# Six small constant tiles allocated ahead of the two token operands, which moves the operands by 224 bytes in every partition

## The chip, the cores and the metric

The kernel runs on one core of one Trainium2 chip. The metric is the device time in microseconds (us) of one execution; the time before is 2092.78 us, the median of three runs from 2089.54 to 2096.44 us.

## What is computed

One transformer block on 256 tokens of width 2048, all in float32: a modulation vector from a conditioning row (`mod = silu(c) @ ada_w + ada_b`, six pieces), a normed and modulated mixer, and a normed and modulated expert layer.

```
h = rms_norm(x, norm_mix_g) * (1 + sc1) + sh1
x = x + gt1 * hybrid_mixer(h, ...)      # attention (3 branches) + gated linear recurrence
h = rms_norm(x, norm_ffn_g) * (1 + sc2) + sh2
x = x + gt2 * peer_ffn(h, ...)          # 16384 experts: gelu(h @ down.T) * gate, then @ up
```

The expert layer of the kernel is dense: it multiplies all tokens with all 16384 rows of `down` and `up` and sets the gates of experts that were not picked to zero.

## The kernel before

**Operands in halves.** A float32 matrix product is made of three float32r products (`mm3`, L345 to L348): both operands are split into a high and a low half (`split`, L196 to L198: ScalarE makes the high half, VectorE the low one), and high times high, high times low and low times high are added up in PSUM. In `T.matmul(o, ah, bh)` the second argument is the stationary operand, which TensorE loads into the array ahead of the product (LDWEIGHTS in the profile), and the third is the moving one, which streams through it. The stationary operand is always a block of 128 tokens: 128 columns of 4 bytes, 512 contiguous bytes in each partition. The moving one is 512 columns of split weights (`wh`, `wl`).

**Two families of stationary tiles.** `xH` and `xL` (L116, L117) hold the halves of what the next product needs of all tokens, 16 chunks of 256 tokens, and are refilled three times: with the first norm's result, the mixer's output and the second norm's result. They are the stationary operands of the first projections (PSUM tiles `f`, `a`, `r`, `xg`), of the mixer's output projection (`y`), of the experts' queries (`wq`) and of the experts' down products (`d`, 32 blocks). The up products (`u`) read other stationary tiles, `ah` and `al` (L1228, L1229), which hold the gated activations of one block of 512 experts; there are four buffers of each.

**The stream.** Weights arrive in the order of one list, a megabyte at a time (`raw`, on SP's queue), are split into `wh` and `wl` and go to TensorE in that order; beside the stream run small jobs, one step per part. A down block is 96 matmuls, an up block 48. The first 14 down blocks run with the search for the picked experts and with the building of their gates (`w`, L1184, eight small matmuls at a time) between their parts; the other 18 down blocks take turns with up blocks and have nothing between.

**Places in SBUF.** The pool `cp` has one buffer per tile, and its tiles lie one behind the other in the order in which they are allocated, each rounded up to 32 bytes per partition. `con`, `sm`, `row`, `cb`, `mod` and `cs` come first, then `xH` and `xL` (16384 bytes per partition each), then `spl`, `nsp` and `hb` (L392 to L394), and the three tiles that `softplus` makes, `e8`, `s8` and `q8` (L397 to L399). In the built program `xH` begins at byte 32576 of each partition and `xL` at 48960; both are 320 modulo 512. Each block of 128 tokens is 512 bytes, so every stationary block of `xH` and `xL` begins at 320 modulo 512. The buffers of `ah` lie from byte 170016 and those of `al` from byte 186400, in steps of 4096: 32 modulo 512, all of them. The buffers of `wh` and `wl` begin at 32 modulo 512 too, but for two of each that serve in the first projections alone and begin at 96.

Of the kernel before, what the change touches and what calls it, by code (L numbers as in the profile page):

```python
# [7 lines left out]
F32 = mybir.dt.float32  # L8
# [7 lines left out]
P = 128  # L16
# [8 lines left out]
RB = 8  # L25
# [40 lines left out]
def kernel(  # L66
# [24 lines left out]
    V, A, T, G = nc.vector, nc.scalar, nc.tensor, nc.gpsimd  # L91
# [22 lines left out]
    mod = cp.tile([P, 6, NDC], F32, name="mod")  # L114
    cs = cp.tile([P, NDC], F32, name="cs")
    xH = cp.tile([P, NDC, S], F32R, name="xH")  # L116
    xL = cp.tile([P, NDC, S], F32R, name="xL")  # L117
# [9 lines left out]

# [1 line left out]
    items = []  # L129
# [11 lines left out]
    for ch in STREAM.replace(" ", ""):  # L141
# [6 lines left out]
        else:  # L148
            src, o = wid[ch].pop(0)
# [27 lines left out]
    def load(most=RAWB):  # L177
        """Loads the stream ahead, as far as the rings allow."""
        while pos["load"] < len(items):
            it = items[pos["load"]]  # L180
            if len(raws) >= most:
                return
            t = wp.tile([P, D], F32, tag="raw", bufs=RAWB, name="raw")
            if it[0] == "ada":
                nc.sync.dma_start(t, ada_w[ada_w.shape[0] - NDC + it[1]])
            elif it[0] == "adp":
                nc.sync.dma_start(t, ada_p[it[1]])
            elif it[0] == "cmp":
                nc.sync.dma_start(t, cmp_w[it[1]][:, it[2] * D:(it[2] + 1) * D])
            else:  # L190
                n = it[2] * it[3]
                nc.sync.dma_start(t[:, 0:n], it[1])
            raws.append(t)
            pos["load"] += 1
# [5 lines left out]
    def ada_load():  # L200
        """Loads ahead, as far as the rings allow."""
        n = pos["adl"]
        if n < ada_w.shape[0] - NDC:
            own = n >= 2 * NDC or n < ADO and n % (ADAB + ADA1) < ADAB
            if sum(o == own for o, _ in avs) < (ADAB if own else ADA1):
                if own:
                    t = vp.tile([P, D], F32, tag="av", bufs=ADAB, name="av")
                else:
                    t = xp.tile([P, D], F32, tag="av1", bufs=ADA1, name="av1")
                nc.sync.dma_start(t, ada_w[n])  # L210
                avs.append((own, t))
                pos["adl"] += 1
                return True
        return False

    def ada(m):
        """One chunk of a modulation vector: rows of the turned weights times the conditioning."""
        t = avs.pop(0)[1]
        V.scalar_tensor_tensor(out=t, in0=t, scalar=1.0, in1=cb, op0=OP.mult, op1=OP.mult, accum_out=m)  # L219
        n = pos["adl"]  # L220
        while (pos["adl"] < 2 * NDC or n - len(avs) > 2 * NDC) and ada_load():
            pass

    def ada_close(seg, k, n):
        """The biases; where it scales, one plus it, times the norm's gain."""
        m = mod[:, seg, k:k + n]
# [7 lines left out]
    def bg(r):  # L234
        """A share r of a chunk of the modulation vectors that VectorE makes beside the rest."""
        bgn[1] += r
# [13 lines left out]
    def adp_item():  # L250
        """A chunk of the rows of one modulation vector, in four column groups of the array."""
        i = items[pos["take"]][1]
# [20 lines left out]
    def next_part():  # L273
        """Emits the next part of the stream; False at its end."""
        if pos["take"] >= (pos["end"] or len(items)):
# [38 lines left out]

# [1 line left out]
    jobs = []  # L316
# [13 lines left out]

    # steps per part of the stream, by the kind of work; the gate build's first steps go as fast as they may
    tk, wn = [0.0], [0]
# [7 lines left out]
    def finish(prio):  # L340
        """Runs the jobs up to that priority to their end."""
        while jobs and jobs[0][0] <= prio:
            step()
# [25 lines left out]
    def rsqrt(pool, ss, n, w, name, parts=P, bufs=2):  # L369
        """1/sqrt(ss/n + eps) of a few columns, by Newton's method from an integer first guess."""  # L370
        v = pool.tile([parts, w], F32, tag="rsv", bufs=bufs, name=f"rsv_{name}")
# [19 lines left out]

    spl = cp.tile([P, RB], F32, name="spl")  # L392
    nsp = cp.tile([P, RB], F32, name="nsp")
    hb = cp.tile([P, 2, RB], F32, name="hb")  # L394

    def softplus():
        e8 = cp.tile([P, RB], F32, name="e8")  # L397
        s8 = cp.tile([P, RB], F32, name="s8")
        q8 = cp.tile([P, RB], F32, name="q8")  # L399
        lam = sm[:, S_LAM:S_LAM + 8]  # L400
# [16 lines left out]

# [1 line left out]
    ea, e0, eq = ExitStack(), ExitStack(), ExitStack()  # L419
# [40 lines left out]
    def ada_first(n):  # L460
        """Chunks of the first two modulation vectors; the tokens' next two chunks when they are complete."""
        for _ in range(n):
# [10 lines left out]

    # two sets of four blocks, in turn over pieces of the width; the sums of the set that rests wait in SBUF
    sums = {"f": [], "a": []}
# [36 lines left out]
    def rest(b, name):  # L512
        """The rest of one of the first four blocks, added up in SBUF."""
        pst = [ps_x(f"{name}_{tb}") for tb in range(NT)]
# [17 lines left out]
    def mix(*gens, rate=0.0):  # L532
        """Steps of several pieces of work in turn."""
        gens = list(gens)
# [7 lines left out]

# [1 line left out]
    ap = ea.enter_context(tc.tile_pool(name="ap", bufs=1))  # L544
# [18 lines left out]
    vc = zp.tile([16, NG, HD], F32, name="vc")  # L563
    # the compressed branch borrows what the later branches fill
    win = oT.rearrange("p h t -> p (h t)").rearrange("p (a l g n) -> p a l g n", a=2, l=32, g=2)
# [3 lines left out]
    def table(i):  # L569
        """The rotation's tables with a norm's gains folded in."""  # L570
        gv = row[:, P * i:P * i + P]
# [8 lines left out]
    def rope(dst, src, nh, cos, sin, name):  # L580
        """dst = src*cos + swap(src)*sin over nh heads of 128."""
        b = tp1.tile([P, nh, 2, 64], F32, tag="ropeb", bufs=1, name=f"rb_{name}")
# [126 lines left out]

# [1 line left out]
    lw = rn.tile([P, 2, RB, P], F32, name="lw")  # L711
    G.dma_start(lw, lru_w)
    def recurrence(gr):
        n = RG
        if True:
# [4 lines left out]
            for c_ in range(n):  # L720
# [13 lines left out]
                A.activation(ta[:, c_], ta[:, c_], AF.Tanh, scale=spl[:, k:k + 1], bias=spl[:, k:k + 1])  # L734
            # d = 1/(1 + tanh) refined from (1 + exp)/2; decay 2d - 1; input sqrt(tanh) d (1 + ti) u
            d = xr[:, :, 0:S]
# [16 lines left out]

# [1 line left out]
    held = {}  # L755

    def scores(sp, g, tb):
        """Unnormed weights of the causal and the windowed branch, and their sums."""
        n = (tb + 1) * P
# [28 lines left out]
    def outputs(sp, g, tb):  # L788
        """The compressed branch's weights; all gated weights turned and times the values."""
        hs = slice(4 * g, 4 * g + 4)  # L790
# [56 lines left out]

# [1 line left out]
    def norm_stats(pool, rbs, o, name, pre=None):  # L849
# [174 lines left out]

# [1 line left out]
    ssr = yp.tile([P, NT], F32, name="ssr")  # L1026
# [22 lines left out]

# [1 line left out]
    bp = ctx.enter_context(tc.tile_pool(name="bp", bufs=1))  # L1051
# [19 lines left out]
    def ev_wq(j, pst):  # L1071
        """Scores of two heads; leaves them to the search."""
        res = []
# [19 lines left out]
    def search(j, tb, sc):  # L1093
        for k in range(4):
            top16(mv[:, tb, 4 * j + k], mi[:, tb, 4 * j + k], sc[:, k * P:(k + 1) * P], P, f"a{j}{tb}{k}")
            yield
        # both lists are sorted: rank (a, b) has (a + 1)(b + 1) - 1 before it, so only those under 16 can be picked
        cd = kq.tile([P, 2, NCD], F32, tag="cd", bufs=2, name=f"cd{j}{tb}")
# [14 lines left out]
    def picks(tb):  # L1113
        """From places in the candidate lists to expert rows, and the softmax; heads and picks on partitions."""
        hi = kq.tile([P, 2, PH, TOPK], U32, tag="hi", bufs=1, name=f"hi{tb}")
# [3 lines left out]
        V.tensor_copy(mf, mi[:, tb])  # L1119
        # place p of rank (a, b): a = max(p / 8 - 1, p / 4 - 6, 0), b = p - min(16 a, 8 a + 8, 4 a + 24)  # L1120
        V.tensor_scalar(hi[:, 0], pk[:, tb], 3, None, OP.logical_shift_right)
# [39 lines left out]
    def w_build():  # L1161
        """Gate weights by expert and token: per token the product of two one-hot tables."""
        stg, ohs, gas, wps = {}, {}, {}, {}
# [27 lines left out]

# [1 line left out]
    xTt, wts, actH, actL = {}, {}, {}, {}  # L1193
# [218 lines left out]
```

## Time and profile before

| what | value |
|---|---|
| median of three runs | 2092.78 us (2089.54 to 2096.44) |
| profiled execution: span from the first to the last instruction | 2090.6 us |
| around the span, against the median of the runs | 2.2 us |
| TensorE (PE) busy | 2025.0 us, 97% |
| VectorE (DVE) busy | 1449.4 us, 69% |
| ScalarE (ACT) busy | 1053.0 us, 50% |
| bytes moved by DMA | 508.73 MB, 243 GB/s in the mean |

The profile gives of the profiled execution its span alone; the table sets it beside the median. Matmuls are pipelined: one that the profile shows as 396 ns long begins while the one before it is still under way, so the pace of a run of matmuls is read from the distance of their starts, not from their durations.

### The profile page before, as it was taken

The numbers are of one execution on the slowest core, as the hardware profiler recorded it, in microseconds if no ns is written. First come the engines' busy times: TensorE is split into PE (matmuls) and PEld (weight loads), VectorE is DVE, ScalarE is ACT, GpSimd is POOL, SyncE is SP. The second block draws the span as 40 slices with busy tenths as digits, with TensorE's granted clock in tenths as the row PEclk, the third lists the DMA queues.
The fourth block names the chain that finished last, engine by engine and source line by source line (L and its number), as shares of the span: only waits on it lengthen the run. The fifth ranks groups of instructions, "written<-read, shape, count | busy, mean of one in ns | idle before, by whom it ended". The sixth has DMA issues, their size and how long they took to land.

```text
span 2090.6 us, 24862 instructions
## 1 busy us (share of the span) xinstructions
PE 2025.0 (97%) x9434; PEld 1635.6 (78%) x9434; DVE 1449.4 (69%) x2149; ACT 1053.0 (50%) x1526; POOL 60.9 (3%) x95
## 2 busy tenths in 40 slices
PE   5999997999999999999999999999999999999998
PEld 4777664877888888887888888888888888888887
DVE  7888999887998666646667766665555555555566
ACT  3544676545456777854444444444444444444443
POOL 0000000000000000001000000000000000000000
PEclk8999998999999999999999999999999999999999
DMA  9897788994556666579777877765555565555563
GB/s 374 333 358 310 264 341 312 347 347 165 174 177 201 226 218 241 203 258 332 253 243 258 294 251 253 247 244 191 191 193 200 200 202 194 200 201 191 194 209 141
DMA packets 75849, 508.73 MB, mean 243 GB/s; under 512 B 8528, under 2 KB 9040, under 8 KB 20176
## 3 DMA queue, kind: packets, MB, share of 16 engines
q1 hardware_dynamic: 63792, 450.50, 60.5%
q0 software_dynamic: 11936, 56.63, 7.6%
q8 instruction: 74, 1.21, 0.2%
q14 instruction: 47, 0.39, 0.1%
HBM read 478.78 MB, written 28.31 MB: 243 GB/s over the span
## 4 chain that ended last, share of the span: by engine, by line
PE 86%; DVE 6%; issue 3%; DMA 3%; ACT 1%; POOL 0%; SPq 0%; DVEq 0%; POOLq 0%; ACTq 0%
PE d L348 11%; PE d L346 11%; PE d L347 11%; PE u L347 10%; PE u L348 10%; PE u L346 10%; PE w L1184 3%; DVE av L219 2%; DVE wl L198 2%; PE wq L346 1%; PE wq L347 1%; PE wq L348 1%; PE a L347 1%; PE a L348 1%; PE a L346 1%
## 5 line engine op out<-in xcount | busy, mean ns | idle before, releaser
L198 DVE TENSOR_TENSOR wl<-raw,wh 128x1024 fp32r<-128x1024 f32 x649 | 789.6, 1222 | 511.8 <-ACT wh L197 511.6
L197 ACT CAST wh<-raw 128x1024 fp32r<-128x1024 f32 x649 | 680.0, 1050 | 777.8 <-PE u L348 334.5
L346 PE MATMUL d<-wh,xH 128*128 128x512 f32 x1024 | 411.2, 402 | 0.0
L347 PE MATMUL d<-wl,xH 128*128 128x512 f32 x1024 | 405.1, 396 | 0.9 <-DVE wl L198 0.9
L348 PE MATMUL d<-wh,xL 128*128 128x512 f32 x1024 | 404.9, 395 | 0.0
L346 PE MATMUL u<-wh,ah 128*128 128x512 f32 x1024 | 402.1, 393 | 0.0
L347 PE MATMUL u<-wl,ah 128*128 128x512 f32 x1024 | 399.4, 390 | 1.3 <-DVE wl L198 1.2
L348 PE MATMUL u<-wh,al 128*128 128x512 f32 x1024 | 399.1, 390 | 0.0
L348 PEld LDWEIGHTS d<-wh,xL 128*128 128x128 f32 x1024 | 192.4, 188 | 45.8
L347 PEld LDWEIGHTS d<-wl,xH 128*128 128x128 f32 x1024 | 192.7, 188 | 43.9 <-DVE wl L198 1.3
L346 PEld LDWEIGHTS d<-wh,xH 128*128 128x128 f32 x1024 | 192.8, 188 | 42.6
L347 PEld LDWEIGHTS u<-wl,ah 128*128 128x128 f32 x1024 | 192.4, 188 | 41.8 <-DVE wl L198 3.0
L348 PEld LDWEIGHTS u<-wh,al 128*128 128x128 f32 x1024 | 192.2, 188 | 40.5
L346 PEld LDWEIGHTS u<-wh,ah 128*128 128x128 f32 x1024 | 192.3, 188 | 39.0
L219 DVE SCALAR_TENSOR_TENSOR av<-av,cb 128x2048 f32<-128x2048 f32 x64 | 146.0, 2285 | 5.4 <-DMA av<-in_ada_w_dram 5.4
L1168 DVE TENSOR_TENSOR oh<-con,idT 128x1024 f32<-128x1024 f32 x64 | 78.3, 1223 | 64.2 <-PE w L1184 64.2
L1189 ACT ACTIVATE oh<-oh,gT 128x128 f32<-128x128 f32 x256 | 83.7, 394 | 34.8 <-DVE oh L1168 34.5
L1256 DVE TENSOR_TENSOR acc<-acc,u 128x512 f32<-128x512 f32 x112 | 71.6, 681 | 0.0
L1184 PEld LDWEIGHTS w<-oh 128*128 128x128 f32 x512 | 65.5, 191 | 4.4
L1184 PE MATMUL w<-oh 128*128 128x128 f32 x512 | 66.6, 275 | 0.0
L346 PE MATMUL y<-wh,xH 128*128 128x512 f32 x128 | 52.1, 409 | 3.6 <-ACT xH L197 3.6
L346 PE MATMUL wq<-wh,xH 128*128 128x512 f32 x128 | 52.5, 410 | 2.5 <-ACT xH L197 2.5
(365 smaller groups left out, 2044.8 us busy)
## 6 DMA issues: line engine op xcount, KB each, us to landing
raw<-in_down_dram SPq DMA_DIRECT2D x128, 1024.0 KB, 5.0
raw<-in_up_dram SPq DMA_DIRECT2D x128, 1024.0 KB, 5.0
av<-in_ada_w_dram SPq DMA_DIRECT2D x64, 1024.0 KB, 7.1
raw<-in_w_a_dram SPq DMA_DIRECT2D x32, 1024.0 KB, 9.4
raw<-in_ada_p_dram SPq DMA_DIRECT2D x16, 1024.0 KB, 7.1
raw<-in_w_out_dram SPq DMA_DIRECT2D x16, 1024.0 KB, 7.9
raw<-in_wq_dram SPq DMA_DIRECT2D x16, 1024.0 KB, 5.0
wd<-stg POOLq DMA_DIRECT2D x8, 2048.0 KB, 8.0
```

The costliest lines, as they stand in the source:

```text
L197: A.copy(dst_h, src)
L198: V.tensor_tensor(dst_l, src, dst_h.bitcast(F32), OP.subtract)
L219: V.scalar_tensor_tensor(out=t, in0=t, scalar=1.0, in1=cb, op0=OP.mult, op1=OP.mult, accum_out=m)
L346: T.matmul(o, ah, bh, start=first, stop=False)
L347: T.matmul(o, ah, bl, start=False, stop=False)
L348: T.matmul(o, al, bh, start=False, stop=last)
L1168: V.tensor_tensor(oh, iota.unsqueeze(1).unsqueeze(1).to_broadcast([P, 4, 2, P]), idT[:, 4 * q:4 * q + 4].unsqueeze(3).to_broadcast([P, 4, ...
L1184: T.matmul(wps[p_][:, k * P:(k + 1) * P], oh[:, k, 1], oh[:, k, 0], start=True, stop=True)
L1189: A.activation(ohs[p_][:, k, 0], ohs[p_][:, k, 0], AF.Copy, scale=gT[:, t:t + 1])
L1256: V.tensor_tensor(a, a, pst[tb], OP.add)
```

## The change

The six tiles `spl`, `nsp`, `hb`, `e8`, `s8` and `q8` are allocated between `cs` and `xH` and no longer behind `xL`. They take 32, 32, 64, 32, 32 and 32 bytes per partition, 224 together, so `xH` begins at byte 32800 and `xL` at 49184: both 32 modulo 512, that is 224 bytes further on or 288 back modulo 512. The pool keeps its size, and every tile but these eight keeps its place. No operation is added or taken away, and the instructions of all five engines stand in the same order with the same waits as before; names differ in their buffer numbers alone. The rest of the diff takes comments and docstrings out, which shifts line numbers.

```
@@ -113,6 +113,13 @@
     cb = cp.tile([P, D], F32, name="cb")
     mod = cp.tile([P, 6, NDC], F32, name="mod")
     cs = cp.tile([P, NDC], F32, name="cs")
+
+    spl = cp.tile([P, RB], F32, name="spl")
+    nsp = cp.tile([P, RB], F32, name="nsp")
+    hb = cp.tile([P, 2, RB], F32, name="hb")
+    e8 = cp.tile([P, RB], F32, name="e8")
+    s8 = cp.tile([P, RB], F32, name="s8")
+    q8 = cp.tile([P, RB], F32, name="q8")
     xH = cp.tile([P, NDC, S], F32R, name="xH")
     xL = cp.tile([P, NDC, S], F32R, name="xL")
...
@@ -389,14 +396,7 @@
             yield
             A.copy(dst[:, j * 512:(j + 1) * 512], bp)
 
-    spl = cp.tile([P, RB], F32, name="spl")
-    nsp = cp.tile([P, RB], F32, name="nsp")
-    hb = cp.tile([P, 2, RB], F32, name="hb")
-
     def softplus():
-        e8 = cp.tile([P, RB], F32, name="e8")
-        s8 = cp.tile([P, RB], F32, name="s8")
-        q8 = cp.tile([P, RB], F32, name="q8")
         lam = sm[:, S_LAM:S_LAM + 8]
```

## Rows read from the trace of the kernel before

**Rows 1.** The page's head, and of its second part the busy tenths of each of 40 equal slices of the span (PEclk is the granted clock of TensorE in tenths, DMA the busy share of the 16 DMA engines).

```profile
span 2090.6 us, 24862 instructions
...
PE   5999997999999999999999999999999999999998
...
DVE  7888999887998666646667766665555555555566
...
PEclk8999998999999999999999999999999999999999
DMA  9897788994556666579777877765555565555563
```

**Rows 2.** The page's chain of work that ended last, by engine.

```profile
PE 86%; DVE 6%; issue 3%; DMA 3%; ACT 1%; POOL 0%; SPq 0%; DVEq 0%; POOLq 0%; ACTq 0%
```

**Rows 3.** Of the groups of instructions over the whole span: the matmuls of one kind of product each (line, engine, output <- moving, stationary; count; busy us, mean ns of one, idle before them), and two groups of weight loads.

```profile
L347 PE MATMUL d<-wl,xH 128*128 128x512 f32 x1024 | 405.1, 396 | 0.9 <-DVE wl L198 0.9
L347 PE MATMUL u<-wl,ah 128*128 128x512 f32 x1024 | 399.4, 390 | 1.3 <-DVE wl L198 1.2
L347 PEld LDWEIGHTS d<-wl,xH 128*128 128x128 f32 x1024 | 192.7, 188 | 43.9 <-DVE wl L198 1.3
L347 PEld LDWEIGHTS u<-wl,ah 128*128 128x128 f32 x1024 | 192.4, 188 | 41.8 <-DVE wl L198 3.0
L347 PE MATMUL y<-wl,xH 128*128 128x512 f32 x128 | 51.6, 403 | 0.0
L347 PE MATMUL wq<-wl,xH 128*128 128x512 f32 x128 | 51.3, 401 | 0.0
L347 PE MATMUL a<-wl,xH 128*128 128x512 f32 x128 | 51.2, 401 | 1.0 <-DVE wl L198 1.0
L347 PE MATMUL f<-wl,xH 128*128 128x512 f32 x96 | 39.9, 416 | 4.0 <-DVE wl L198 3.8
L347 PE MATMUL r<-wl,xH 128*128 128x512 f32 x32 | 13.4, 418 | 0.0
L347 PE MATMUL xg<-wl,xH 128*128 128x512 f32 x32 | 12.9, 404 | 0.0
```

**Rows 4.** The timeline of TensorE inside a down block: the first and the last of 73 matmuls that follow one another (start us, us, engine line, output <- moving, stationary), and behind them the groups of the same stretch with their counts (25, 24 and 24).

```profile
1229.13 0.40 PE L348 MATMUL d<-wh,xL 128*128 128x512 f32 x1
...
1245.93 0.40 PE L348 MATMUL d<-wh,xL 128*128 128x512 f32 x1
...
L348 PE MATMUL d<-wh,xL 128*128 128x512 f32 x25 | 9.9, 395 | 0.0
L346 PE MATMUL d<-wh,xH 128*128 128x512 f32 x24 | 9.5, 396 | 0.0
L347 PE MATMUL d<-wl,xH 128*128 128x512 f32 x24 | 9.5, 396 | 0.0
```

**Rows 5.** The same inside an up block just before it: the first and the last of 69 matmuls, and the groups of that stretch (three of 23).

```profile
1209.56 0.39 PE L346 MATMUL u<-wh,ah 128*128 128x512 f32 x1
...
1224.97 0.39 PE L348 MATMUL u<-wh,al 128*128 128x512 f32 x1
...
L346 PE MATMUL u<-wh,ah 128*128 128x512 f32 x23 | 8.9, 389 | 0.0
L347 PE MATMUL u<-wl,ah 128*128 128x512 f32 x23 | 8.9, 389 | 0.0
L348 PE MATMUL u<-wh,al 128*128 128x512 f32 x23 | 8.9, 389 | 0.0
```

**Rows 6.** The timeline of TensorE where small matmuls have just come between: in an early down block the 2nd and the 12th matmul behind the gate build; in an up block the 2nd and the 12th behind one set of transposes, and the 2nd and the 12th behind the next.

```profile
693.05 0.40 PE L347 MATMUL d<-wl,xH 128*128 128x512 f32 x1
...
695.37 0.39 PE L348 MATMUL d<-wh,xL 128*128 128x512 f32 x1
...
1255.08 0.40 PE L347 MATMUL u<-wl,ah 128*128 128x512 f32 x1
...
1257.39 0.40 PE L348 MATMUL u<-wh,al 128*128 128x512 f32 x1
...
1258.30 0.40 PE L347 MATMUL u<-wl,ah 128*128 128x512 f32 x1
...
1260.59 0.39 PE L348 MATMUL u<-wh,al 128*128 128x512 f32 x1
```

**Rows 7.** Busy time by stage: the stretch in us, its length, then busy us and count of instructions of PE, PEld (weight loads), DVE, ACT and POOL, the granted clock, the DMA share and GB/s.

```profile
0.00:205.00 205.00, 175.49 (x712) 138.10 (x713) 166.77 (x212) 89.88 (x128) 0.99 (x6) 0.94 0.88 346
205.00:375.00 170.00, 149.87 (x879) 101.05 (x878) 162.17 (x385) 112.80 (x259) 2.84 (x4) 0.94 0.80 309
375.00:500.00 125.00, 117.20 (x524) 94.03 (x524) 106.14 (x146) 63.16 (x88) 4.90 (x9) 0.96 0.81 301
500.00:650.00 150.00, 150.00 (x704) 122.45 (x703) 141.10 (x507) 73.29 (x89) 1.07 (x2) 1.00 0.54 179
650.00:960.00 310.00, 309.13 (x1644) 261.26 (x1643) 187.68 (x168) 224.32 (x456) 16.40 (x28) 1.00 0.64 230
1200.00:2091.00 891.00, 884.62 (x3926) 722.41 (x3924) 513.22 (x533) 384.25 (x406) 17.39 (x22) 1.00 0.61 206
```

**Rows 8.** What TensorE waited for in the first 205 us: total us, number of waits, longest.

```profile
PE f L346 <- ACT xH L197: 16.7, 2, 15.4
PE cb L441 <- DVE s L405: 4.3, 1, 4.3
PE f L347 <- DVE wl L198: 3.8, 2, 2.2
PE a L346 <- ACT wh L197: 1.8, 2, 1.6
```

## The prediction

> **What bounds the kernel now.** I read the page's head and its slices first: the reader is to see PE at 9 tenths in nearly every slice, VectorE near that only in the first quarter, and DMA near full there too [rows 1]. The chain of waits says the same: 86% of the span is PE [rows 2]. So I looked for what sets the pace of PE, and here the view that counts is the timeline, from start to start, since durations overlap.
>
> Inside a down block 73 matmuls start between 1229.13 and 1245.93 us [rows 4]: 16.80 us over 72 distances, 233.3 ns each. Inside the up block before it 69 start between 1209.56 and 1224.97 us [rows 5]: 15.41 us over 68 distances, 226.6 ns each. Both have the same shape, the same buffers of `wh` and `wl` as moving operand, no wait and a granted clock of 1.00 (2.4 GHz; the last stage of [rows 7]). A down matmul thus costs 6.7 ns more than an up matmul, and this holds for the whole span: durations average 396 ns in `d` and 390 in `u` [rows 3]. What differs between the two is the stationary operand alone: `xH`, `xL` at 320 modulo 512, `ah`, `al` at 32. The change puts the first pair at 32 modulo 512, where the second lies. The weight loads themselves are shown as equally long in both, 188 ns [rows 3], so the difference is not in their duration, only in the pace.
>
> **The change part by part.**
>
> *What it moves.* No instruction is added, removed or reordered, so the sum has one kind of term: number of matmuls with `xH` or `xL` as stationary operand, times the nanoseconds that each one's start comes earlier. The number, three groups for each product [rows 3]: `d` 3 x 1024 = 3072, `y`, `wq` and `a` 3 x 128 = 384 each, `f` 288, `r` and `xg` 96 each: 4704 together. The six small tiles are read and written by a few instructions of 8 or 16 columns, in the same places of the order; I cost their move at nothing. The gate logits, where `xH` is the moving operand, are 48 short matmuls; also nothing.
>
> *What the offset is worth.* The trace of before shows no matmul of this kind with `xH` at 32, so I bound the value from both sides: 0 ns if the pace belongs to something else, 6.7 ns if it belongs to the offset [rows 4, 5]. A loss is bounded by a step of the same size the other way, 6.7 ns, the only step between two paces that the trace shows. I take 6.6 ns where nothing comes between (the nearest row is `u` itself, with the same offset modulo 512 in both operands that `d` will have), a little under the full step for the first matmuls of each block.
>
> *Late down blocks (from 1200 us).* 18 blocks x 96 = 1728 matmuls x 6.6 ns = 11.4 us. PE is busy 884.6 of 891 us there and waits for nothing; DVE has 58%, ACT 43%, DMA 61% [rows 7], so the faster PE can be fed, and all of it shortens the end.
>
> *Early down blocks (600 to 960 us), 1344 matmuls.* Here the gate build comes between every 12 matmuls. Behind such a break neither family is at its steady pace: `d` goes from 693.05 to 695.37, 232 ns over ten distances; `u` behind transposes from 1255.08 to 1257.39, 231 ns, and behind the next set 1258.30 to 1260.59, 229 ns [rows 6]. So of about 914 matmuls between breaks (the blocks from 650 to 930 us) each gains between 1 and 3 ns by these rows; bounds 0 and 6.7; I take 2: 1.8 us. The other 430 are unbroken: x 6.6 = 2.8 us. PE is busy 309.1 of 310 us [rows 7].
>
> *Queries.* 384 `wq` matmuls with few breaks: 5 ns, 1.9 us. DVE has 141 of 150 us there [rows 7]; it has to keep ahead of a PE that is 2% faster, which leaves 6% of room.
>
> *Output projection.* 384 `y` matmuls are worth 2.5 us at the full step. PE has 117.2 of 125 us, DVE 106.1, DMA 0.81 and near full in the slice at 420 us [rows 1, 7]. I take half, 1.3 us; bounds 0 and 2.5.
>
> *First projections.* 672 `f` and `a` matmuls are worth 4.4 us. But DMA has 0.88 at 346 GB/s and DVE 166.8 of 205 us [rows 7], and PE waits 16.7 us for `xH` and for split weights after that [rows 8]: where DVE or the transfers set the pace, an earlier PE waits longer. I take 40%, 1.8 us; bounds 0 and 4.4.
>
> *`r` and `xg` (205 to 375 us).* DVE has 162.2 of 170 us [rows 7]; of 1.3 us I take 0.3.
>
> *Sum.* 11.4 + 1.8 + 2.8 + 1.9 + 1.3 + 1.8 + 0.3 = 21.3 us, of a ceiling of 4704 x 6.7 = 31.5 us. The profiled span of 2090.6 us becomes 2069.3; with the 2.2 us that the median of the runs lies above that span: 2071.5 us, 1.0% faster.
>
> **What the notes say against it.** Rows 4 and 5 show two paces for two stationary operands. The Trainium skill, in TensorE: Matmul & The Clock Gate, under what happens when a matmul is issued (step by step), says that the array has two read ports of its own, and that loading the next weights takes no read bandwidth from the running matmul; and in SBUF — State Buffer, under its specifications, that lines are 16 bytes long. By these an operand's place should not matter, as both 320 and 32 are the start of a line, and the sum would be 0. No run here shows ports or lines; the two paces weigh more.
>
> **The rivals.**
>
> *The pace is not the offset's (no change, 2092.8 us).* The down blocks' operands also lie elsewhere (bytes 32576 to 65344 of a partition against 170016 to 202784) and are larger tiles, and the weight loads show the same 188 ns [rows 3]. If one of these sets the pace, everything stays. Against it: nothing else reads or writes that stretch while a block runs, and each block of 512 bytes is laid out alike in both. This is also what the cited rule would give. 13%.
>
> *Half of it comes (2081 us).* The step is gained only where nothing breaks the run: 11.4 us of the late blocks, and in the first 960 us the earlier PE only waits longer for DVE and for the transfers, or a longer wait lets the granted clock fall once more. For it: DVE is at 95% from 205 to 375 us, the clock has 0.94 to 0.96 in three stages [rows 7]. Against it: from 500 us PE is at 100% of each stage. 15%.
>
> *The new place is slower (2118 us).* The pace goes by how stationary and moving operand lie to each other, and with bits above the 512. The trace shows that a place can cost a step of 6.7 ns; if the new one costs another such step in `d`, `y` and `wq` (3840 matmuls), that is 25.7 us more. It decides from some 940 matmuls on (940 x 6.7 = 6.3 us, 0.3%). Against it: `u` has the same two offsets modulo 512 and is the faster one, and its buffers of `ah` and `al`, eight places, all show 389 ns [rows 5]. 5%.
>
> **How the numbers follow.** The forecast as worked out has 67%, half of it 15%, no change 13%, slower 5%. The predicted time is the first, 2071.5 us. Its ends: 4704 x 6.7 gives 2061, the late blocks alone 2081. Cutting off the tail of no change above and allowing a few us of spread between runs (the three lie 7 us apart): 2062 to 2087 us. About 0.3%, 6 us, is what a measurement of this kernel can tell from no change. Faster by more: 67 + 15, less a little for a half gain that comes out small: 81%. Within: 14%. Slower: 5%.
>
> **What would show it.** Right: in the timeline of a late down block 73 matmuls take 16.3 us and not 16.8, their mean is 389 ns and not 396; the weight loads stay at 188; `u` does not change; a down block at 1200 us and later takes 21.8 us and not 22.4. In the early blocks `d` shows about 230 ns between breaks. In the first 375 us the waits of PE for `xH` and `wl` grow by a few us. Wrong: `d` at 396 ns as before (no change), or `d` at 389 but the span shorter by less than 10 us, with the lost time in new waits or in a lower PEclk.

## The result: 0.9911 of the time before, and the profile after

The changed kernel takes 2074.12 us (median of four runs, 2072.49 to 2077.41); the kernel before took 2094.19 us beside it. The ratio is 0.9911, 95% interval 0.9893 to 0.9930: faster by 0.9%; the medians lie 20 us apart. The profiled span went from 2090.6 to 2071.7 us.

The page's head and two of its rows; as in [rows 1], a digit is the tenth of a slice of the span.

```profile
span 2071.7 us, 24862 instructions
PE   5999997998999999999999999999999999999998
PEclk7999998999999999999999999999999999999999
```

Little looks different here: PE is as full as before, and the clock was lowered in nearly the same slices, in the first one a little more (7 for 8). The groups of matmuls (lines are 7 higher now, L347 of before is L354) show where the time went:

```profile
L354 PE MATMUL d<-wl,xH 128*128 128x512 f32 x1024 | 399.5, 390 | 0.5 <-DVE wl L205 0.4
L354 PE MATMUL u<-wl,ah 128*128 128x512 f32 x1024 | 399.2, 390 | 1.9 <-DVE wl L205 1.7
L354 PEld LDWEIGHTS d<-wl,xH 128*128 128x128 f32 x1024 | 192.6, 188 | 39.1 <-DVE wl L205 1.7
L354 PE MATMUL y<-wl,xH 128*128 128x512 f32 x128 | 50.7, 396 | 0.0
L354 PE MATMUL wq<-wl,xH 128*128 128x512 f32 x128 | 50.6, 395 | 0.0
L354 PE MATMUL a<-wl,xH 128*128 128x512 f32 x128 | 50.7, 397 | 1.9 <-DVE wl L205 1.9
L354 PE MATMUL f<-wl,xH 128*128 128x512 f32 x96 | 40.0, 417 | 5.3 <-DVE wl L205 5.1
```

`d` has come down from 396 ns to the 390 of `u` [rows 3], `u` and the weight loads have not moved, `y`, `wq` and `a` lost 4 to 7 ns each; `f` nothing. The timeline inside a late down block, first and last of 72 matmuls, and the groups of the stretch, as in [rows 4]:

```profile
1221.80 0.39 PE L355 MATMUL d<-wh,xL 128*128 128x512 f32 x1
...
1237.89 0.39 PE L354 MATMUL d<-wl,xH 128*128 128x512 f32 x1
```

```profile
L355 PE MATMUL d<-wh,xL 128*128 128x512 f32 x24 | 9.3, 389 | 0.0
L353 PE MATMUL d<-wh,xH 128*128 128x512 f32 x24 | 9.3, 389 | 0.0
L354 PE MATMUL d<-wl,xH 128*128 128x512 f32 x24 | 9.3, 389 | 0.0
```

16.09 us over 71 distances, 226.6 ns against 233.3 [rows 4]: the pace of `u` [rows 5]. Which stage gave what is read from the starts of the five kinds of product (count: duration ns least/median/most, then the first and the last start in us):

```profile
L353 PE MATMUL f<-wh,xH x96: 387/394/793, 35.6 to 161.2; 128*128 128x512 f32 x96
L353 PE MATMUL y<-wh,xH x128: 387/389/793, 367.4 to 464.8; 128*128 128x512 f32 x128
L353 PE MATMUL wq<-wh,xH x128: 387/389/795, 475.9 to 572.7; 128*128 128x512 f32 x128
L353 PE MATMUL d<-wh,xH x1024: 388/389/485, 573.3 to 1998.7; 128*128 128x512 f32 x171
L353 PE MATMUL u<-wh,ah x1024: 387/389/478, 954.4 to 2065.0; 128*128 128x512 f32 x171
```

The same five in the trace of before:

```profile
L346 PE MATMUL f<-wh,xH x96: 388/396/796, 34.0 to 160.3; 128*128 128x512 f32 x96
L346 PE MATMUL y<-wh,xH x128: 392/396/793, 365.9 to 465.8; 128*128 128x512 f32 x128
L346 PE MATMUL wq<-wh,xH x128: 392/396/796, 476.7 to 575.4; 128*128 128x512 f32 x128
L346 PE MATMUL d<-wh,xH x1024: 389/395/482, 576.1 to 2017.6; 128*128 128x512 f32 x171
L346 PE MATMUL u<-wh,ah x1024: 387/389/478, 962.1 to 2083.9; 128*128 128x512 f32 x171
```

And in a second trace of the changed kernel, taken beside the last of the experiments (span 2071.5 us); it shows how far one trace can be trusted for a single stage:

```profile
L353 PE MATMUL f<-wh,xH x96: 388/394/796, 33.5 to 157.9; 128*128 128x512 f32 x96
L353 PE MATMUL y<-wh,xH x128: 387/389/792, 364.2 to 461.6; 128*128 128x512 f32 x128
L353 PE MATMUL wq<-wh,xH x128: 387/389/796, 472.7 to 569.5; 128*128 128x512 f32 x128
L353 PE MATMUL d<-wh,xH x1024: 388/389/481, 570.1 to 1998.5; 128*128 128x512 f32 x171
L353 PE MATMUL u<-wh,ah x1024: 387/389/478, 952.7 to 2064.8; 128*128 128x512 f32 x171
```

The differences give the stages:

| stage | before, us | after, us | gained | second trace, us | gained | forecast |
|---|---|---|---|---|---|---|
| up to the first `f` | 34.0 | 35.6 | -1.6 | 33.5 | 0.5 | none |
| `f` to `y` (first projections, mixer) | 331.9 | 331.8 | 0.1 | 330.7 | 1.2 | 2.1 |
| `y` to `wq` | 110.8 | 108.5 | 2.3 | 108.5 | 2.3 | 1.3 |
| `wq` to `d` | 99.4 | 97.4 | 2.0 | 97.4 | 2.0 | 1.9 |
| first `d` to first `u` (early down blocks) | 386.0 | 381.1 | 4.9 | 382.6 | 3.4 | 4.6 |
| first `u` to last `u` (late down blocks) | 1121.8 | 1110.6 | 11.2 | 1112.1 | 9.7 | 11.4 |

The matmuls of the first two stages are quicker too: distances of `a` and `f` without a wait average 228 to 230 ns after and 233 before. In the first trace nothing of it shows at the start of `y`, in the second 1.7 us do. The two traces part early. The stretch from 40 to 60 us, before, after, and in the second trace (columns as in [rows 7]; the granted clock is the third figure from the end):

```profile
40.00:60.00 20.00, 17.11 (x72) 13.12 (x72) 17.36 (x19) 8.71 (x13) 0.00 (x0) 1.00 0.96 373
40.00:60.00 20.00, 17.33 (x64) 13.59 (x63) 18.10 (x21) 6.24 (x10) 0.00 (x0) 0.83 0.93 344
40.00:60.00 20.00, 17.09 (x74) 13.37 (x73) 17.43 (x20) 9.24 (x14) 0.00 (x0) 1.00 0.97 363
```

In the first trace PE waits 2.7 us for a low half there (1.6 us in the other two), and the clock falls to 1.2 GHz in that wait and stays there for part of the stretch. Matmul by matmul this trace falls 1.2 us back between 45 and 55 us; the second does not.

### The profile page after: what moved, and what is told of

It is laid out like the page before. It is cut to its first block, busy times and chain, and to the rows that moved or that the text cites. A ratio compares the mean times of both kernels' runs of the same rounds, so it can differ in the third digit from the quotient of the medians.

```text
span 2071.7 us, 24862 instructions
## 1 busy us (share of the span) xinstructions
PE 2003.6 (97%) x9434; PEld 1635.3 (79%) x9434; DVE 1448.5 (70%) x2149; ACT 1053.0 (51%) x1526; POOL 60.9 (3%) x95
## 4 chain that ended last, share of the span: by engine, by line
PE 76%; DVE 11%; issue 9%; DMA 2%; ACT 2%; POOL 1%; SPq 0%; DVEq 0%; POOLq 0%; ACTq 0%
PE d L353 10%; PE d L355 10%; PE d L354 10%; PE u L355 8%; PE u L354 8%; PE u L353 8%; DVE wl L205 3%; DVE av L226 3%; PE w L1184 3%; PE y L353 1%; PE y L355 1%; PE y L354 1%; PE xt L1207 1%; PE wq L353 1%; PE wq L354 1%
## 5 line engine op out<-in xcount | busy, mean ns | idle before, releaser
L353 PE MATMUL d<-wh,xH 128*128 128x512 f32 x1024 | 406.3, 397 | 0.0
L354 PE MATMUL u<-wl,ah 128*128 128x512 f32 x1024 | 399.2, 390 | 1.9 <-DVE wl L205 1.7
L354 PE MATMUL d<-wl,xH 128*128 128x512 f32 x1024 | 399.5, 390 | 0.5 <-DVE wl L205 0.4
L355 PE MATMUL d<-wh,xL 128*128 128x512 f32 x1024 | 399.4, 390 | 0.0
L354 PEld LDWEIGHTS u<-wl,ah 128*128 128x128 f32 x1024 | 192.4, 188 | 41.7 <-DVE wl L205 3.1
L354 PEld LDWEIGHTS d<-wl,xH 128*128 128x128 f32 x1024 | 192.6, 188 | 39.1 <-DVE wl L205 1.7
```

The source lines that it names most:

```text
L353: T.matmul(o, ah, bh, start=first, stop=False)
L354: T.matmul(o, ah, bl, start=False, stop=False)
L355: T.matmul(o, al, bh, start=False, stop=last)
```

## The experiments

A first reading of the result would be that the address of a stationary block sets the pace. Eleven runs ask what about the address. Offsets are places in bytes modulo 512 in a partition; distances are from start to start in the blocks from 1200 us on, means over those without a break, from the trace. Each ratio is to the kernel before on the same chip.

**All sixteen distances in one run.** A chunk of `xH` and `xL` takes 32 bytes more, so the sixteen chunks lie at sixteen places:

```
-    xH = cp.tile([P, NDC, S], F32R, name="xH")
+    xH = cp.tile([P, NDC, S + 8], F32R, name="xH")[:, :, 0:S]
...
-            rw = wp.tile([P, 512], F32, tag="adr", bufs=1, name="adr")
+            rw = adpool[0].tile([P, 512], F32, tag="tab", bufs=1, name="adr")
```

(`xL` alike; the second edit makes room.)

> Each of the 16 chunks of xH and xL is 8 columns (32 bytes) further from the one before than now, so that the stationary blocks of chunk k begin at 32 + 32 k modulo 512: all sixteen multiples of 32 in one run. Theory A (the place of the stationary block in a line of 64 bytes decides: odd multiples of 32 are fast, multiples of 64 slow): in the late down blocks chunks with even k keep 226.7 ns from start to start, odd k take 233.3; the mean is 230 and the time 2084 us. Theory B (it decides how near the block lies to the moving tile's 32 modulo 512): chunk 0 alone is at 226.7, most others at 233.3, time 2092 us. Theory C (a boundary inside 512 is crossed or not): a contiguous range of k is fast and the rest slow.

2093.64 us in its single run. The mean of the three distances of a chunk (high-high, high-low, low-high):

| chunk k, k + 8 | 0, 8 | 1, 9 | 2, 10 | 3, 11 | 4, 12 | 5, 13 | 6, 14 | 7, 15 |
|---|---|---|---|---|---|---|---|---|
| chunk k, ns | 228.2 | 231.9 | 233.4 | 232.8 | 233.0 | 233.6 | 230.4 | 233.7 |
| chunk k + 8, ns | 231.1 | 232.9 | 233.4 | 232.8 | 233.1 | 233.6 | 230.4 | 233.8 |

Not A (even chunks 2, 4, 10 and 12 stand at 233 ns like the odd ones), not C (no unbroken range is short). Chunk 0 is the quickest, as B has it; it also stands right behind an up block at the short pace. But from the third column on the two rows agree within 0.1 ns: the pattern comes again after eight chunks, 256 bytes, and in the mean of both rows the first pair is the quickest. A chunk is only six matmuls long, so no pace is steady here; the next runs hold one place over whole blocks.

**xL alone back at 320.**

```
-    (six small tiles)
-    xH = cp.tile(...)
     xL = cp.tile(...)
+    (six small tiles)
+    xH = cp.tile(...)
```

> xL comes ahead of the six small tiles and xH behind them: xL begins at 320 modulo 512 as in the kernel before, xH at 32 as in the changed one; no other tile moves. If each matmul's distance goes by the place of the weights that are loaded for it or beside it, one distance in three is long: in the late down blocks 226.7, 226.7 and 233.3 in turn, mean 228.9, and the time 2074 + 20/3 = 2081 us. If the whole stream falls into one pace by its slowest load: 233.3 throughout and 2094 us.

2091.92 us, ratio 0.9988 (0.9977 to 0.9999): nearly all of the gain is lost by a third of the weight loads. The timeline of a down block (start us, us, ...):

```profile
1240.21 0.40 PE L353 MATMUL d<-wh,xH 128*128 128x512 f32 x1
1240.44 0.40 PE L354 MATMUL d<-wl,xH 128*128 128x512 f32 x1
1240.68 0.39 PE L355 MATMUL d<-wh,xL 128*128 128x512 f32 x1
1240.91 0.40 PE L353 MATMUL d<-wh,xH 128*128 128x512 f32 x1
```

Three distances now differ, 232, 239 and 228 ns on average, but three together take 0.70 us, 233.3 each, as before. Of the two outcomes in the expectation the second is right in the mean, and near in the time: one load in three out of line costs nearly as much as all three.

**ah and al at 320.**

```
-            acc = upp.tile([P, NT, D], F32, name="acc")
+            acc = upp.tile([P, NT * D + 72], F32, name="acc")[:, 0:NT * D].rearrange(...)
```

> The changed kernel with 288 unused bytes ahead of the tiles of the up products: ah and al begin at 320 modulo 512 and xH, xL at 32. If the place of a stationary block decides for any product: u goes from 226.7 to 233.3 ns, 3072 x 6.6 = 20 us more, 2094 us. If the long pace was a property of xH and xL alone (their size, their part of the partition): no change, 2074 us.

2092.69 us, ratio 0.9993 (0.9982 to 1.0003). Now it is `u` that is slow:

```profile
L354 PE MATMUL u<-wl,ah 128*128 128x512 f32 x1024 | 405.3, 396 | 0.8 <-DVE wl L205 0.8
L354 PE MATMUL d<-wl,xH 128*128 128x512 f32 x1024 | 399.5, 390 | 0.6 <-DVE wl L205 0.4
```

Distances 233.2 in `u`, 226.7 in `d`. The long pace is no property of `xH` and `xL`.

**Everything at 320.** In the kernel before, 288 bytes behind the six tiles:

```
-        q8 = cp.tile([P, RB], F32, name="q8")
+        q8 = cp.tile([P, RB + 72], F32, name="q8")[:, 0:RB]
     (adr moved as above)
```

> xH and xL stay at 320 as in the kernel before, and 288 bytes more behind them move every later tile (the moving wh and wl, and ah and al) from 32 to 320 modulo 512; one scratch row goes into a tile that is free by then, to make room. Stationary and moving lie to each other as in the changed kernel, at another place. If the place itself decides (theory A or C): d and u both at 233.3 ns, 4704 + 3072 matmuls at the long pace, 2094 + 20 = 2114 us. If the lie of the two to each other decides (theory B): d and u both at 226.7 ns, 2074 us.

2074.52 us, ratio 0.9906 (0.9887 to 0.9924), as fast as the changed kernel, with `xH` and `xL` where they were before:

```profile
L347 PE MATMUL d<-wl,xH 128*128 128x512 f32 x1024 | 399.9, 391 | 1.2 <-DVE wl L198 1.1
L347 PE MATMUL u<-wl,ah 128*128 128x512 f32 x1024 | 399.7, 390 | 2.4 <-DVE wl L198 2.3
```

226.7 ns in `d` and, as in the changed kernel, 227.3 in `u` (its first matmuls behind each set of transposes are slower). So 320 is not slow by itself, and theories A and C, which had it slow, fall for good. What counts is how stationary and moving operand lie to each other (theory B).

**Single distances, held over whole blocks.** `xH`, `xL` on one hand and `ah`, `al` on the other are moved by so many bytes from `wh` and `wl`, in three kernels:

```
-    xH = cp.tile([P, NDC, S], F32R, name="xH")
+    xH = cp.tile([P, NDC * S + 128], F32R, name="xH")[:, q:q + NDC * S].rearrange(...)
     (xL alike; ah and al alike with another q)
```

> xH and xL begin at 64 modulo 512 (32 bytes further than wh and wl), ah and al at 96 (64 bytes further). If only the exact same place modulo 512 gives the short pace: d and u at 233.3 ns, 2114 us. If the places need to agree modulo 64 alone: u short (226.7), d long, 2094 us. If a small distance is enough: both short, 2074 us.

> xH and xL begin at 0 modulo 512 (32 bytes ahead of wh and wl), ah and al at 288 (256 further). If only the same place modulo 512 is short: both at 233.3, 2114 us. If the places must agree modulo 256: u short, d long, 2094 us. If a small distance on this side is enough: d short.

> xH and xL begin at 48 modulo 512 (16 bytes further than wh and wl), ah and al at 160 (128 further). If only the same place modulo 512 is short: both at 233.3, 2114 us. If the places must agree modulo 128: u short, d long, 2094 us. If 16 bytes do not matter: d short.

| kernel | `d` at, distance ns | `u` at, distance ns | us | ratio (95%) |
|---|---|---|---|---|
| first | +32: 233.3 | +64: 233.4 | 2112.56 | 1.0104 (1.0075 to 1.0134) |
| second | -32: 233.3 | +256: 227.3 | 2092.40 | 1.0010 (0.9996 to 1.0025) |
| third | +16: 233.0 | +128: 233.2 | 2104.72 | 1.0068 (1.0046 to 1.0091) |

The groups of the second in one stretch (1275 to 1320 us) show both paces side by side; the count is that of the stretch:

```profile
L354 PE MATMUL d<-wl,xH 128*128 128x512 f32 x32 | 12.6, 395 | 0.0
...
L354 PE MATMUL u<-wl,ah 128*128 128x512 f32 x32 | 12.5, 390 | 0.0
```

256 bytes apart is as good as the same place (227.3 in the changed kernel); 16, 32, 64, 128 and -32 are not. The third run is quicker than 2114 us in part because its stream leaves the long pace now and then: `u` averages 232.4 ns between 1000 and 1200 us and 233.2 later, `a` and `f` 231 in the first 205 us. That is about half of the difference, an estimate from these paces; the rest is not explained. Why at 16 or 128 and not at 32 or 64 was not tried further.

**Agreement modulo 256, mixed modulo 512.** `xH` at 288, `xL` at 32, `ah` and `al` at 288, `wl`'s buffers at 288, 32 and 288:

```
-        wl = pool.tile([P, 2, 512], F32R, ...)
+        wl = pool.tile([P, 1088], F32R, ...)[:, 64:1088].rearrange("p (k n) -> p k n", k=2)
     (xH, xL as above with 64 of 64 more columns)
```

> Every place differs from its partner's by a whole multiple of 256 bytes, but they are not the same modulo 512: xH at 288, xL at 32, ah and al at 288, wh at 32, the three buffers of wl at 288, 32 and 288. If it is agreement modulo 256 that gives the short pace: d and u at 226.7 ns throughout, about 2074 us. If the half by 256 was an accident of ah and al alone, or if all must be the same modulo 512: both at 233.3 ns, up to 2114 us.

2073.15 us, ratio 0.9904 (0.9882 to 0.9926); 226.7 ns in `d` and 227.3 in `u`, both as in the changed kernel. Modulo 256 is enough.

**Which pair has to agree.** In the timeline of the changed kernel each load starts with the matmul before its own (the load for a `wh`, `xH` product at 1229.96 us, where the `wh`, `xL` matmul ahead of it starts too); so the low halves alone are moved:

```
     wl, xL, al: 72 columns (288 bytes) further; wh, xH, ah stay
```

> The low halves of all three kinds (wl, xL, al) are moved to 320 modulo 512, the high halves (wh, xH, ah) stay at 32. TensorE loads the stationary tile of a product while the product before it streams: ah during a stream of wh, al during a stream of wl. Theory B1 (the weights being loaded must lie as the operand that streams beside them): every load then matches, d and u at 226.7 ns, 2074 us. Theory B2 (a stationary operand must lie as its own moving operand): one product in three matches, or all stationary operands must lie alike as the run with xL alone at 320 suggests: d and u at 233.3 ns, 2114 us.

2101.96 us, ratio 1.0053 (1.0030 to 1.0076): `d` and `u` at 233.3, 231.5 and 231.9 ns in turn, 232.2 in the mean. Neither theory holds whole: agreement of each load with the stream beside it doesn't bring the short pace (B1 falls), but the pace is a little under the long one and the time 12 us under B2's 2114, which no run here explains. The short pace was held only where all four operands of the stream agree modulo 256.

**The rest of TensorE's operands, too.** `con`, the gate build's tables and the first projections' extra weight buffers to 32 modulo 256:

```
-    con = cp.tile([P, C_END], F32, name="con")
+    con = cp.tile([P, C_END + 128], F32, name="con")[:, 40:40 + C_END]
...
-                oh = kq.tile([P, 4, 2, P], F32, tag="eq", bufs=3, name=f"oh{q}")
+                oh = kq.tile([P, 1088], F32, tag="eq", bufs=3, name=f"oh{q}")[:, 48:1072].rearrange(...)
     (eq in the picks alike; sc16 48 columns longer)
```

> The changed kernel with the other operands of TensorE brought to 32 modulo 256 too: the split weights' extra buffers of the first projections (from 96), the identity (from 128), the one-hot tables of the gate build (from 96). If small matmuls at other places are what puts the stream out of its short pace after each break: the early down blocks go from 229.5 to 226.7 ns, first projections from 229 to 227, together 3 to 5 us, 2070 us. If the break itself does it, whatever its place: no change from the kernel run beside it, within 2 us.

> The changed kernel once more, on the same chip, to set the last one against: 2074 us.

2073.95 us, ratio 0.9903 (0.9887 to 0.9919), against 2073.49, ratio 0.9908 (0.9892 to 0.9923): no difference. The paces did move: between 700 and 900 us the down blocks' distances went from 229.7 to 228.3 ns, in the first 200 us from 228.9 to 227.0. Behind a gate build the stream is at 227 ns after three matmuls and not after seven; the timeline of the 2nd to 5th and of the 12th matmul there:

```profile
691.35 0.40 PE L354 MATMUL d<-wl,xH 128*128 128x512 f32 x1
691.58 0.39 PE L355 MATMUL d<-wh,xL 128*128 128x512 f32 x1
691.81 0.39 PE L353 MATMUL d<-wh,xH 128*128 128x512 f32 x1
692.04 0.39 PE L354 MATMUL d<-wl,xH 128*128 128x512 f32 x1
...
693.63 0.39 PE L355 MATMUL d<-wh,xL 128*128 128x512 f32 x1
```

2.28 us over ten distances, 228 ns. That is 1.4 ns for some 914 matmuls, 1.3 us, under what these runs can tell apart; and in the profiled run the granted clock was 0.983 against 0.987, which may have taken it back. None of the versions tried beats the changed kernel measurably.

## Why the prediction was right, step by step

**The pace.** Right: 6.6 ns for each matmul with `xH` or `xL`, read from the pace of `u`. Its reason needs mending. The prediction spoke of the offset modulo 512; the runs show that the offset is nothing by itself (everything at 320 is fast) and that agreement with the moving operands modulo 256 is what counts. That the number came out all the same was luck in this point: `wh` and `wl` were at 32 already, so the place of `ah` and `al` was also the place that agrees. The rival with the slower outcome had named just this mechanism, how the two operands lie to each other, but with bits above the 512 and the new place on the wrong side. Two readings were loose without harm: [rows 5] shows one stretch of `u`, not eight places (over the whole trace of before the median of the 1024 `u` above is 389 ns), and an up block is 96 matmuls, not 48 (24, 12 and 60 of them stand between two late down blocks).

**Late down blocks** 11.4, measured 11.2 us, and 9.7 in the second trace, whose stage begins with more waiting (below). From 1213 us on, where PE waits for nothing, the lead over the kernel before grows by 11.6 us in both traces, matmul by matmul. **Queries** 1.9, measured 2.0.

**Early down blocks** 4.6, measured 4.9 and 3.4. About 1.2 us of the 4.9 are not the pace: in the last down block PE waits 0.9 us for a low half before, and 1.2 us in the second trace, but not in the first. Behind a gate build the changed kernel needs, from the 2nd to the 12th matmul, this long:

```profile
693.17 0.39 PE L354 MATMUL d<-wl,xH 128*128 128x512 f32 x1
...
695.47 0.39 PE L355 MATMUL d<-wh,xL 128*128 128x512 f32 x1
```

2.30 us over ten distances, 230 ns against 232 [rows 6]: the 2 ns that were taken from `u`'s behaviour behind transposes.

**Output projection** 1.3, measured 2.3, but about half of that is the clock. In the kernel before, TensorE stood at 1.2 GHz for the first 5.4 us of this stage, in the changed one for 3.2 us. From 355 to 375 us, before and after:

```profile
355.00:375.00 20.00, 13.67 (x67) 11.57 (x67) 16.68 (x37) 10.52 (x16) 2.84 (x4) 0.66 0.90 354
355.00:375.00 20.00, 13.68 (x76) 11.72 (x75) 17.75 (x38) 11.80 (x18) 2.84 (x4) 0.74 0.88 331
```

2.2 us at half the clock are worth 1.1 us, an estimate from these figures, which leaves 1.2. A run with the low clock of the changed kernel and the long pace bears it out: the second of the kernels with single distances (`y` at 233.3 ns, 3.1 us at 1.2 GHz) takes 109.9 us from `y` to `wq` against 108.5, 1.4 us more. The forecast of half was right.

**First projections, `r` and `xg`** 2.1, measured 0.1 and 1.2. The step that failed is the 40%, together with a clock that the sum left out. The waits did grow, and took more than the prediction gave them:

```profile
PE f L353 <- ACT xH L204: 15.4, 1, 15.4
PE f L354 <- DVE wl L205: 5.1, 2, 2.7
```

The second was 3.8 us before [rows 8]. The first was to grow as well and fell from 16.7; its 15.4 us lie ahead of the first `f`, where no faster matmul can reach. All waits of PE from 40 to 206 us together are 7.9 us before, 8.8 after and 9.1 in the second trace: about 1 us more, not the whole gain. The clock is the other part. Between the first `f` and the first `y` TensorE stood at 1.2 GHz for 28 us in the kernel before, for 31 us in the first trace and for 27 us in the second. At half the clock that is worth up to 1.6 us against the first trace and 0.6 us for the second, so that by this estimate 0.6 to 1.7 us were the pace's own, less than the 2.1. The first `f` is 1.6 us later in the first trace and 0.5 us earlier in the second: spread between runs. With it 21.3 us became 18.9 in the profiled span, 19.1 in the second.

**What the sum left out.** It adds up the stages as if each one's gain reached the end. The two traces of the changed kernel show that an early gain need not: the second is 3.2 us ahead of the first at 940 us, matmul by matmul, and 0.3 us at 1000 us. The waits of PE between 940 and 1010 us, first trace, then second:

```profile
PE u L354 <- DVE wl L205: 0.7, 1, 0.7
...
PE u L354 <- DVE wl L205: 2.0, 3, 1.2
PE d L354 <- DVE wl L205: 1.2, 1, 1.2
```

The trace that came to this stretch earlier waited longer for the split weights. So the 1.2 us that the second trace has gained on the first projections hardly shortened its end: the two spans differ by 0.2 us.

**The rivals.** No change falls with the result. The Trainium skill (TensorE: Matmul & The Clock Gate, step by step) says that loading the next weights takes no read bandwidth from the running matmul; here their place relative to the moving operand cost 6.6 ns a matmul, and the measurement decides. Half of it falls too: that rival kept nothing of the first 960 us, but 7.7 us were gained up to the first `u` (9.4 in the second trace), and 7.3 and 7.5 of them were left at 1213 us. What it named, longer waits and a lower clock, did take part of the early gain.

## What to carry to other kernels

Where a long run of 512-column float32r matmuls is the bound, compare the distance from start to start between products whose operands lie differently; 224 bytes of other tiles in front were worth 6.6 ns in 233 here (no other shape was tried). Give stationary tiles and the moving tiles beside them the same place modulo 256 in a partition, all of them: one of four that lies otherwise took back nearly everything. The cheapest way is to allocate small tiles so that the large ones behind them start alike; nothing in the order of instructions shows the difference. And take a second trace before a stage's gain of 1 or 2 us is explained: two traces of this same kernel differ by as much.

## What the runs showed of the hardware that was not expected

At a granted clock of 1.00 a stream of loads and matmuls held 226.7 ns where all operands agree modulo 256, and 233.3 ns in most runs where one or more do not; 232.2 ns (low halves alone moved) and 232.4 to 233.2 (16 and 128 bytes) were seen too. With `xL` alone out of line the single distances are 232, 239 and 228 ns and still sum to three times 233.3. Weight loads are shown as 188 ns long in either case, so a load's own duration does not tell which pace it is; a matmul's does (389 and 396 ns). After a break by small matmuls the stream needs about seven matmuls to find the short pace, three in the run in which the small ones' operands lie alike too. What it is in the memory or the array that has a period of 256 bytes no run here shows, and why the pace wavers at 16, 128 and 192 bytes stays open.
